# Four operand tiles of an FFN's Strassen products moved by 960 bytes: a longer pad at the end of their pool

## The chip, the cores and the metric

The kernel runs on one core of a Trainium2 chip. The metric is the device time of one execution in microseconds. Three executions of the kernel before took 2714.53, 2717.65 and 2718.61 us; the median, 2717.65 us, is the time that the changed kernel is compared with.

## What is computed

One decoder block in float32: a mixer (sliding-window attention and an mLSTM branch side by side, merged by gates) and a SwiGLU feed-forward network, each behind a modulated RMS norm. The sequence has 2048 tokens of width 1024; the feed-forward width is 2816. The change concerns the first two products of the feed-forward part, `h2 @ w_ffn_gate` and `h2 @ w_ffn_up`:

```
h2 = modulate(rms_norm(x, g_pre_ffn[l]), shift_f, scale_f)
ff = (jax.nn.silu(h2 @ w_ffn_gate[l]) * (h2 @ w_ffn_up[l])) @ w_ffn_down[l]
x = x + gate_f[:, None, :] * rms_norm(ff, g_post_ffn[l])
```

## The kernel before

**Products.** A float32 value is split into a high part (rounded to fp32r by a cast on ScalarE, line 1358) and a low part (the rest, a subtraction on VectorE, line 1359). Each product of two float32 blocks then takes three matmuls: high by high, high by low, low by high.

**Strassen.** The large products are done in Winograd's form of Strassen's method, with seven block products in place of eight. `PROD` (line 1337) lists them as pairs of a weight block and an activation block: ("11","11"), ("S3","T3"), ("S2","T2"), ("22","T4"), ("S1","T1"), ("12","21"), ("S4","22"). S1 to S4 are sums of weight blocks, made on VectorE while the weights are prepared (`a_operands`, lines 1438 to 1466: three sums, lines 1450 to 1452, with the first product of a pair, and S4, line 1461, with the last). T1 to T4 are sums of activation blocks, made once for 1024 tokens by `h_combine` (lines 1380 to 1426), which also splits them.

**The feed-forward part.** Tokens are taken in two halves of 1024 (`b2` = 0 and 1). For each half, `gate_up` (line 1551) runs over eleven pairs of feature tiles, and for each pair over the gate weights and then the up weights; `pair_parts` (line 1468) issues the seven products of one such pair. Each product has four steps of depth 128, and each step three matmuls:

```
for kk in range(4):
    l, r = (hi[:, kk, :], lo[:, kk, :]), tuple(t[:, kk, :] for t in HC[B])
    mm(ps, l[0], r[0], kk == 0 and i in (0, 1, 5), False, True)
    mm(ps, l[0], r[1], False, False, True)
    mm(ps, l[1], r[0], False, kk == 3, True)
```

So a product is 12 matmuls. The weights (`hl`, a double tile of high and low part) are the stationary operand, loaded by TensorE's weight load; the activation rows, 512 float32 or 2048 bytes in each of 128 partitions, are the moving operand. Products 11, S2·T2, S1·T1 and S4·22 add up in a PSUM bank named `acc`, the others in one named `mix`. After a half's `gate_up`, `down` (line 1618) multiplies by `w_ffn_down`; there both operands are `hl` tiles.

**Where the activation blocks lie.** `HC` holds a high and a low tile for each of the seven blocks, `[P, 4, TB]` each: 8192 bytes in each partition, four rows of 2048 bytes. The tiles of 11, 21, 22, T1 and T3 come from the pool `bpool` (name `big`), those of T2 and T4 from a pool of their own, `hcp`, which `open_hc` (line 1364) opens at the right end of SBUF when the mixer's last pool there is closed. Their names are `hcT2h`, `hcT2l`, `hcT4h` and `hcT4l`. Both halves use the same four tiles: they are filled before the first `gate_up`, and again during `down` of the first half. A last small tile, `hc_end`, only takes up room: a pool at the right end grows downwards, so its length sets where the four tiles lie. In the built program they start at bytes 196544, 204736, 212928 and 221120 of a partition, each of which is a multiple of 1024 plus 960. The tiles `big` start at 43008 and every 8192 bytes from there, the tiles `hl` at 26624 and every 4096 bytes from there: all multiples of 1024.

The queues that matter here are TensorE's (matmuls in the order of `PROD`), ScalarE's and VectorE's (splits of the weights up to four products ahead, `ahead=4` in line 1490, and the combination of results in lines 1495 to 1505) and SyncE's, which issues the DMAs.

Of the kernel before, what the change touches and what calls it, by code (L numbers as in the profile page):

```python
# [10 lines left out]
F32 = mybir.dt.float32  # L11
# [8 lines left out]
P = 128  # L20
# [51 lines left out]
def decoder_block(ctx: ExitStack, tc: tile.TileContext, a: dict, out: bass.AP, dbg=None):  # L72
# [664 lines left out]
    def superblock(sb):  # L737
# [475 lines left out]
        def outputs(b):  # L1213
# [24 lines left out]
            def before_m():  # L1238
                end_chunks(NT * (b % 2 + 1))
                load_y(b, 2)  # L1240
                if b + 1 == NBLK:
                    finish(R_ada)
                    open_hc()
                    R["hc"] = spawn(h_combine(0, *HC_FROM_MIXER), L_HC)
# [119 lines left out]
    def open_hc():  # L1364

        p1k.close()
        hcp = ctx.enter_context(tc.tile_pool(name="hcp", bufs=1, side="right", reuse_waits="tile"))
        HC.clear()
        t2h, t2l, t4h, t4l = [hcp.tile([P, 4, TB], F32R, name=f"hc{x}") for x in ("T2h", "T2l", "T4h", "T4l")]
        hcp.tile([P, 8], F32, name="hc_end")  # L1370
        HC["T2"] = [t2h, t2l]
        HC["T4"] = [t4h, t4l]

# [487 lines left out]
```

## Time and profile before

| | us |
|---|---|
| median of three executions | 2717.65 |
| the profiled execution | 2714.22 |
| its span, from the first to the last instruction | 2712.5 |
| TensorE busy in the span | 2641.9 |
| VectorE busy | 1955.8 |
| ScalarE busy | 1303.1 |
| first product with a T2 tile starts at | 1422.0 |
| last matmul with a T4 tile starts at | 2481.5 |

The span is 1.7 us shorter than the profiled execution's own time; the rest lies around it. "Busy" is the time in which an engine had at least one instruction under way. Matmuls overlap: the profile shows a duration for each that is longer than the time until the next one starts, so a run of matmuls is measured from the start of its first to the start of the first one behind it.

### The profile page before, as it was taken

How to read it: one execution, taken by the hardware profiler on the slowest of the kernel's cores; microseconds unless marked ns; L12 is line 12 of the kernel's file. 1: busy time of each engine (PE TensorE's matmuls, PEld its weight loads, DVE VectorE, ACT ScalarE, POOL GpSimd, SP SyncE). 2: the span in 40 equal slices, each digit the busy share in tenths (PEclk: the TensorE clock that was granted, in tenths of full speed). 3: DMA queues.
4: the chain of work that ended last, by engine and by line, in shares of the span. 5: the costliest groups of instructions: out<-in, count | busy, mean ns of one | idle time of the engine just before them, and what ended most of it. 6: DMA issues, size and time to landing. Idle time of an engine off the chain costs nothing.

```text
span 2712.5 us, 35701 instructions
## 1 busy us (share of the span) xinstructions
PE 2641.9 (97%) x12310; PEld 2141.0 (79%) x12310; DVE 1955.8 (72%) x3818; ACT 1303.1 (48%) x2574; POOL 157.8 (6%) x189
## 2 busy tenths in 40 slices
PE   6999999999999999999999999999999999999998
PEld 4867788888886778888878888888777888888886
DVE  7967787777696877776687777776676666666466
ACT  5646544444855654454554433334554333333444
POOL 2010001100101000110000000000000000000000
PEclk8999999999999999999999999999999999999999
DMA  7655346887675643678764454446685232224566
GB/s 250 201 174 172 128 139 200 260 341 253 214 234 161 198 147 119 216 236 300 239 208 166 171 202 149 161 158 223 206 273 184 98 117 95 99 97 148 184 213 217
DMA packets 353638, 511.89 MB, mean 189 GB/s; under 512 B 25120, under 2 KB 213660, under 8 KB 348208
## 3 DMA queue, kind: packets, MB, share of 16 engines
q1 hardware_dynamic: 353456, 509.61, 56.0%
q8 instruction: 97, 1.59, 0.2%
q14 instruction: 85, 0.70, 0.1%
HBM read 357.12 MB, written 144.02 MB: 185 GB/s over the span
## 4 chain that ended last, share of the span: by engine, by line
PE 83%; DVE 8%; DMA 4%; ACT 3%; issue 1%; SPq 0%; POOL 0%; DVEq 0%; ACTq 0%; POOLq 0%
PE acc L204 58%; PE mix L204 24%; PE mix L209 2%; DVE hl L1359 1%; ACT tm L948 1%; DMA raw<-as_d 1%; ACT hl L1358 1%; DMA raw<-in_w_in_dram 1%; DMA big<-big 1%; DVE tm L428 1%; DMA raw<-ws_d 0%; DMA at_d<-tx 0%; DVE big L1359 0%; DVE wlo L260 0%; DMA big<-in_x_dram 0%
## 5 line engine op out<-in xcount | busy, mean ns | idle before, releaser
L204 PE MATMUL acc<-big,hl 128*128 128x512 f32 x3936 | 946.3, 393 | 3.7 <-DVE w L1658 1.7
L204 PEld LDWEIGHTS acc<-big,hl 128*128 128x128 f32 x3936 | 732.7, 188 | 172.5 <-issue 11.4
L1358 ACT CAST hl<-raw 128x512 fp32r<-128x512 f32 x732 | 436.0, 620 | 615.2 <-PE acc L204 384.3
L1359 DVE TENSOR_TENSOR hl<-raw,hl 128x512 fp32r<-128x512 f32 x732 | 494.8, 695 | 255.8 <-ACT hl L1358 249.7
L204 PE MATMUL acc<-whi,big 128*128 128x512 f32 (+1 forms) x1280 | 382.6, 379 | 15.3 <-ACT big L518 8.4
L204 PEld LDWEIGHTS acc<-whi,big 128*128 128x128 f32 x1280 | 237.7, 193 | 59.2 <-ACT big L518 8.5
L204 PE MATMUL mix<-big,hl 128*128 128x512 f32 x1056 | 270.6, 392 | 1.7 <-DVE hl L1359 1.0
L204 PE MATMUL acc<-wlo,big 128*128 128x512 f32 (+1 forms) x640 | 242.6, 381 | 2.8 <-DVE wlo L260 2.8
L204 PE MATMUL acc<-hl,hl 128*128 128x512 f32 x1008 | 237.7, 393 | 6.2 <-DVE hl L1359 3.9
L204 PEld LDWEIGHTS mix<-big,hl 128*128 128x128 f32 x1056 | 198.9, 189 | 45.7 <-DVE hl L1359 1.8
L204 PEld LDWEIGHTS acc<-hl,hl 128*128 128x128 f32 x1008 | 187.0, 188 | 51.9 <-DVE hl L1359 9.3
L204 PE MATMUL mix<-hl,hl 128*128 128x512 f32 x792 | 182.5, 391 | 1.1 <-DVE hl L1359 0.4
L204 PEld LDWEIGHTS mix<-hl,hl 128*128 128x128 f32 x792 | 147.8, 188 | 34.9 <-DVE hl L1359 2.8
L260 DVE TENSOR_TENSOR wlo<-raw,whi 128x1024 fp32r<-128x1024 f32 (+1 forms) x96 | 108.8, 1135 | 69.1 <-ACT whi L259 64.1
L204 PE MATMUL acc<-big,whi 128*128 128x512 f32 x512 | 157.2, 392 | 0.0
L259 ACT CAST whi<-raw 128x1024 fp32r<-128x1024 f32 (+1 forms) x96 | 94.3, 983 | 124.4 <-PE acc L204 108.2
L475 POOL TENSOR_TENSOR rs<-ms,nhalf 128x1 f32<-128x1 f32 (+1 forms) x56 | 53.0, 958 | 1603.1 <-DVE ms L473 1598.0
L204 PEld LDWEIGHTS acc<-wlo,big 128*128 128x128 f32 x640 | 124.0, 194 | 25.6 <-DVE wlo L260 4.2
L204 PE MATMUL acc<-hcT2h,hl 128*128 128x512 f32 x352 | 117.6, 394 | 1.2 <-ACT w L1499 1.2
L204 PE MATMUL mix<-hcT4h,hl 128*128 128x512 f32 x352 | 117.5, 394 | 0.0
L204 PEld LDWEIGHTS acc<-big,whi 128*128 128x128 f32 x512 | 95.7, 188 | 19.5
L204 PE MATMUL acc<-big,wlo 128*128 128x512 f32 x256 | 97.9, 393 | 0.0
(324 smaller groups left out, 3423.3 us busy)
## 6 DMA issues: line engine op xcount, KB each, us to landing
raw<-in_w_in_dram SPq DMA_DIRECT2D x48, 1024.0 KB, 5.4
as_d<-w SPq DMA_DIRECT2D x154, 256.0 KB, 2.0
raw<-as_d SPq DMA_DIRECT2D x70, 512.0 KB, 4.0
raw<-in_w_ffn_gate_dram SPq DMA_DIRECT2D x22, 1024.0 KB, 5.2
raw<-in_w_ffn_up_dram SPq DMA_DIRECT2D x22, 1024.0 KB, 5.8
raw<-ws_d SPq DMA_DIRECT2D x40, 512.0 KB, 4.6
y_d<-tm SPq DMA_DIRECT2D x64, 256.0 KB, 5.5
tx<-in_w_ada_dram SPq DMA_DIRECT2D x64, 256.0 KB, 4.5
```

The costliest lines, as they stand in the source:

```text
L204: T.matmul(o, lhsT=lhsT, rhs=rhs, start=start, stop=stop, skip_group_check=resumed)
L209: T.transpose(o, i, ident[:k, :k])
L259: A.copy(hv, src)
L260: V.tensor_tensor(lv, src, hv.bitcast(F32), op=ALU.subtract)
L428: V.scalar_tensor_tensor(acc, raw[:, k, :], c_, acc, op0=ALU.mult, op1=ALU.add)
L475: G.tensor_tensor(r[:, :n], ms[:, :n], nhalf[:, :n], op=ALU.pow)
L948: A.activation(sc[g][:, j, :], sc[g][:, j, :], AF.Exp, bias=nm_[:, hd:hd + 1], accum_out=sums[:, hd:hd + 1])
L1358: A.copy(v(hi), src)
L1359: V.tensor_tensor(v(lo), src, v(hi).bitcast(F32), op=ALU.subtract)
```

## The change

`hc_end`, the last tile of the pool `hcp`, has 248 float32 per partition in place of 8: 992 bytes in place of 32. Nothing reads or writes it. The four tiles ahead of it start 960 bytes lower, at 195584, 203776, 211968 and 220160, which are multiples of 1024. These four addresses are the only difference between the two built programs: each engine has the same instructions in the same order with the same waits, and all other tiles and the tensors in HBM lie where they lay.

```
@@ -1367,7 +1367,7 @@
         hcp = ctx.enter_context(tc.tile_pool(name="hcp", bufs=1, side="right", reuse_waits="tile"))
         HC.clear()
         t2h, t2l, t4h, t4l = [hcp.tile([P, 4, TB], F32R, name=f"hc{x}") for x in ("T2h", "T2l", "T4h", "T4l")]
-        hcp.tile([P, 8], F32, name="hc_end")
+        hcp.tile([P, 248], F32, name="hc_end")
         HC["T2"] = [t2h, t2l]
         HC["T4"] = [t4h, t4l]
```

More of the change, by code (lines that the diff above doesn't have):

```diff
@@ L1369, in open_hc @@
         t2h, t2l, t4h, t4l = [hcp.tile([P, 4, TB], F32R, name=f"hc{x}") for x in ("T2h", "T2l", "T4h", "T4l")]
-        hcp.tile([P, 8], F32, name="hc_end")
+        hcp.tile([P, 248], F32, name="hc_end")
         HC["T2"] = [t2h, t2l]
```

## The prediction

> **What bounds the kernel now.** I read the page's busy times first, then the chain that ended last, then the two stretches in which the moved tiles are used, and last the tiles themselves. The first two views:
>
> ```profile
> span 2712.5 us, 35701 instructions
> PE 2641.9 (97%) x12310; PEld 2141.0 (79%) x12310; DVE 1955.8 (72%) x3818; ACT 1303.1 (48%) x2574; POOL 157.8 (6%) x189
> ...
> PE 83%; DVE 8%; DMA 4%; ACT 3%; issue 1%; SPq 0%; POOL 0%; DVEq 0%; ACTq 0%; POOLq 0%
> ```
>
> TensorE is busy for 97% of the span and holds 83% of the chain. An average over stages does not say what holds where the change acts, so the next view takes the two stretches of gate and up products alone (the T2 and T4 tiles are moving operands there and nowhere else), and the one after it lists what a matmul waited for in the first of them.
>
> ```profile
> core 0: us, PE busy (x) PEld busy (x) DVE busy (x) ACT busy (x) POOL busy (x), PEclk, DMA share, GB/s
> 1422.00:1829.00 407.00, 407.00 (x1778) 333.48 (x1779) 294.07 (x469) 156.08 (x282) 13.00 (x4) 1.00 0.47 167
> 2072.00:2482.00 410.00, 410.00 (x1793) 335.91 (x1792) 276.80 (x430) 145.96 (x259) 0.34 (x1) 1.00 0.32 108
> ```
>
> ```profile
> engine line waited for: us in total, times, longest us
> PE acc L204 <- ACT w L1499: 1.2, 1, 1.2
> ```
>
> The reader is to see three things. TensorE is busy for every microsecond of both stretches, at a granted clock of 1.00. Its only wait in the first is 1.2 us at the very start. VectorE, the next busiest, works 294.07 us of 407.00. These 817 us are thus bound by the rate at which matmuls follow each other, and by nothing else that the trace shows.
>
> **What sets that rate.** The tile views give the durations of matmuls by moving operand (least, median, most, in ns).
>
> ```profile
> L204 PE MATMUL acc<-hcT2h,hl x352: 393/394/502, 1422.0 to 2478.7; 128*128 128x512 f32 x176
> L204 PE MATMUL acc<-hcT2l,hl x176: 392/394/398, 1422.3 to 2478.4; 128*128 128x512 f32 x176
> L204 PE MATMUL mix<-hcT4h,hl x352: 393/394/398, 1424.9 to 2481.5; 128*128 128x512 f32 x176
> L204 PE MATMUL mix<-hcT4l,hl x176: 393/394/398, 1425.1 to 2481.2; 128*128 128x512 f32 x176
> ...
> L204 PE MATMUL acc<-big,hl x3936: 387/389/796, 209.8 to 2490.9; 128*128 128x512 f32 x197
> L204 PE MATMUL mix<-big,hl x1056: 387/389/628, 1408.6 to 2486.9; 128*128 128x512 f32 x176
> L204 PE MATMUL acc<-hl,hl x1008: 387/389/504, 1835.3 to 2691.9; 128*128 128x512 f32 x168
> L204 PE MATMUL mix<-hl,hl x792: 387/389/501, 1870.2 to 2672.1; 128*128 128x512 f32 x198
> ```
>
> All eight groups have the same shape, type and stationary tile. Four have a median of 389 ns and a least of 387; the four whose moving operand is a T2 or T4 tile have 394 and 392 to 393. Not one of the 1056 on T tiles is as short as the median of the others: this is no scatter. What tells the four apart is where the tile lies: `big` and `hl` start at multiples of 1024 bytes, the T tiles 960 bytes past one. Durations overlap, though, and their ends are modelled, so I take the price from starts. The chain over one pair of gate or up weights merges matmuls that follow each other into the same bank name (start, length, count):
>
> ```profile
> 1458.01 2.80 PE acc L204 x12
> 1460.80 5.09 PE mix L204 x22
> 1465.89 2.72 PE acc L204 x12
> 1468.61 0.45 PE mix L204 x2
> 1469.07 2.72 PE acc L204 x12
> 1471.79 0.45 PE mix L204 x2
> 1472.24 2.72 PE acc L204 x12
> 1474.96 2.27 PE mix L204 x10
> 1477.22 2.80 PE acc L204 x12
> ```
>
> The first piece is S2·T2, the second S22·T4 with ten matmuls on T3's or 21's tiles behind it; the third, fifth and seventh are the products of `acc` on `big` tiles. Twelve matmuls on T2 take 2.80 us, or 233.3 ns each; twelve on `big` take 2.72 us, or 226.7 ns each. The second piece agrees: 5.09 less 2.27 for ten on `big` (the eighth piece) leaves 2.82 us for the twelve on T4. The second half's stretch shows the same lengths at the same places:
>
> ```profile
> 2108.82 2.27 PE mix L204 x10
> 2111.09 2.80 PE acc L204 x12
> 2113.89 5.09 PE mix L204 x22
> ```
>
> **The change part by part.**
>
> *The matmuls on the T tiles.* They are 352 + 176 + 352 + 176 = 1056, or 88 products of 12 (two halves, eleven pairs, gate and up, T2 and T4). At multiples of 1024 I expect them to run like the `big` and `hl` tiles, which lie so: 88 x (2.80 - 2.72) = 88 x 0.08 = **7.0 us less**. With the rounding of both lengths (0.07 to 0.09) that is 6.2 to 7.9 us; by the modelled durations, 1056 x (394 - 389) ns = 5.3 us. At the other end, if the price belongs to something that the move leaves alone (the pool, the far end of SBUF), it is nothing. I take 7.0, since starts are recorded and ends modelled, and since the 6792 matmuls of the other four rows, on tiles at multiples of 1024, agree with each other.
>
> By a rule of the Trainium skill it would be nothing: "TensorE: Matmul & The Clock Gate", section "Wait — 56ns, not 53.3ns?", gives the time from one bf16 matmul to the next, back to back and warm, as the columns over 2.4 GHz and some 2.5 ns more, 215.7 ns at 512, with no term for the operand's address. The trace agrees with it on neither tile group: 226.7 and 233.3 ns stand beside it, in fp32r, and the two differ.
>
> *What lies beside it.* The matmuls follow each other without a wait, so the whole of it is on the path. To be late next, VectorE or ScalarE would have to need more than TensorE: a pair takes 1477.22 - 1458.01 = 19.21 us now and 19.05 after; VectorE's part of it is 294.07 / 407.00 x 19.21 = 13.9 us, ScalarE's 156.08 / 407.00 x 19.21 = 7.4 us, and the DMA engines are at 0.47. Gate and up weights are asked for once in that time, so a pair that is 0.16 us shorter moves no transfer into another's way. If VectorE's cover of 5 us were gone, nothing of the 7.0 us would be left, since TensorE would then run at VectorE's pace.
>
> *The writes into the T tiles.* These are 16 casts and 16 subtractions, 8 of each for each half:
>
> ```profile
> L1358 ACT CAST hcT2h<-tx x4: 613/619/623, 1346.8 to 1383.9; 128x512 fp32r<-128x512 f32 x4
> L1359 DVE TENSOR_TENSOR hcT2l<-tx,hcT2h x4: 681/686/691, 1350.3 to 1386.0; 128x512 fp32r<-128x512 f32 x4
> ...
> L1358 ACT CAST hl<-raw x732: 602/622/654, 208.2 to 2687.5; 128x512 fp32r<-128x512 f32 x183
> L1359 DVE TENSOR_TENSOR hl<-raw,hl x732: 659/687/1524, 209.5 to 2688.2; 128x512 fp32r<-128x512 f32 x183
> ```
>
> A write to a T tile takes what a write to an `hl` tile takes (619 against 622 ns, 686 against 687), so I cost it at nothing. Were all 32 in the path and each moved by the whole 3 ns, it would be 0.1 us either way.
>
> *The weight loads.* Their stationary tiles do not move. The load runs beside the matmul ahead of it:
>
> ```profile
> L204 PEld LDWEIGHTS acc<-hcT2h,hl x352: 186/187/188, 1422.0 to 2478.4; 128*128 128x128 f32 x176
> ...
> L204 PEld LDWEIGHTS acc<-big,hl x3936: 186/188/333, 209.8 to 2490.7; 128*128 128x128 f32 x197
> ```
>
> Beside a matmul of 226.7 ns a load of 188 ns keeps some 39 ns of cover (46 now); nothing comes of it.
>
> *The rest.* The pad is neither read nor written. Instructions, waits and all other addresses stay, so `down`, the mixer and every DMA are as before; they only start earlier, by 3.5 us behind the first half and by 7.0 us behind the second.
>
> **The sum.** The profiled execution goes from 2714.22 to 2707.2 us, its span from 2712.5 to 2705.5. That execution lay 3.4 us under the median of the three, 2717.65; from the median the forecast is **2710.6 us**, 0.26% less. About 0.2% (5.4 us) is what a measurement of this kernel can tell from no change.
>
> **The rivals.**
>
> *The address is not the cause: no change, 2717.65 us.* The T tiles differ from `big` in more than the remainder by 1024: they lie in a pool of their own above all other tiles. If the 6.7 ns belong to that, they stay. For it speaks that no row shows one tile at both kinds of address. Against it, `hl`, from byte 26624, and `big`, up to byte 157696, run alike to the nanosecond, which a price that grows with the address would not leave. The Trainium skill's page "SBUF — State Buffer" stands on this side: "Specifications (TRN2)" names lines of 16 bytes as the grain, and both the old and the new addresses are multiples of 64. "Who interferes with whom" adds that TensorE waits for no other engine there. No row here shows the size of a line.
>
> *The time comes free and is waited away: 2714 to 2717 us.* Place: the hand-over from a product to the splits that later ones need, and then `down`, which waits for DMAs at many places. If one of the two stretches turned out to follow VectorE's or the DMAs' pace, half would be lost: 2717.65 - 3.5 = 2714.1 us. The 407.00 and 410.00 us of unbroken work speak against it.
>
> *The new place collides: slower.* At multiples of 1024 the T tiles share that remainder with the `hl` tiles, which TensorE's weight load reads, and ScalarE and VectorE write, in the same moments. If meeting there cost a matmul as much on top of its present time as the old place costs it, 6.7 ns, the 1056 would give 7.0 us more: 2724.7 us. It decides from 5.4 us / 1056 = 5.1 ns over the present 233.3, that is, where twelve matmuls take over 2.86 us. Against it stands that the `big` tiles share the remainder and the neighbours already, and run at 2.72.
>
> **How the numbers follow.** The forecast gets 0.80, no effect of the address 0.09, gain waited away 0.08, the collision 0.03. The three runs of before lie 4.1 us apart, and the forecast only 1.6 us past the bound of 5.4: of its 0.80 I count 0.05 to "within 0.2%". That gives faster 0.75, same 0.05 + 0.09 + 0.08 = 0.22, slower 0.03. The range goes from the fastest run of before less the largest gain, 2714.53 - 7.9 = 2706.6 us, to the slowest less half the forecast, 2718.61 - 3.5 = 2715.1 us; it takes in most of the waited-away case, and leaves out no effect and the collision, 0.12, with some tails of the forecast.
>
> **What the profile after would show.** Right: the four rows of T2 and T4 at a median of 389 ns and a least of 387; pieces of twelve on T2 of 2.72 us, and of 22 in `mix` of 5.01; both stretches still unbroken and shorter by 3.5 us each. The first is wrong if the rows stay at 394 (the address is not the cause) or rise (collision). The second is wrong if the rows fall to 389 and the pair stays at 19.21 us, with new idle time of TensorE before the splits of lines 1358 and 1359. The forecast of the time is wrong, with all of that right, if `down` gives back more than a microsecond or two in waits for its loads.

## The result and the profile after

The changed kernel took 2706.86 us, the median of six runs (2704.91 to 2708.56), against 2716.30 us for six runs of the kernel before (2711.73 to 2718.61). The ratio is 0.9966, with a 95% interval of 0.9953 to 0.9979: 0.34% faster, or 5.7 to 12.8 us. The profiled execution took 2706.42 us, 7.8 us less than the one of before. One execution of a later run, the one with the pad at 56, took 5071.58 us at a granted clock of 0.89, where the seven others had 0.99, and its ratio and median leave it out.

The head of the page after:

```profile
span 2704.7 us, 35701 instructions
...
PE 2630.0 (97%) x12310; PEld 2139.2 (79%) x12310; DVE 1953.4 (72%) x3818; ACT 1303.3 (48%) x2574; POOL 149.1 (6%) x189
```

The span is 7.8 us shorter, and TensorE's share of it is 97% as before: it does the same 12310 matmuls faster. The chain still runs through TensorE for the most part (82%, before 83%). The matmuls with a moved tile, from the tile views (least, median, most in ns; first and last start in us):

```profile
L204 PE MATMUL acc<-hcT2h,hl x352: 387/389/504, 1421.7 to 2471.0; 128*128 128x512 f32 x176
L204 PE MATMUL acc<-hcT2l,hl x176: 389/389/402, 1422.0 to 2470.8; 128*128 128x512 f32 x176
L204 PE MATMUL mix<-hcT4h,hl x352: 389/389/390, 1424.6 to 2473.7; 128*128 128x512 f32 x176
L204 PE MATMUL mix<-hcT4l,hl x176: 389/389/390, 1424.8 to 2473.5; 128*128 128x512 f32 x176
```

All four medians fell from 394 to 389 ns, the number of the `big` and `hl` tiles. The chain over one pair, as it was shown of before:

```profile
1457.37 2.72 PE acc L204 x12
1460.09 4.99 PE mix L204 x22
1465.08 2.72 PE acc L204 x12
1467.80 0.45 PE mix L204 x2
1468.25 2.72 PE acc L204 x12
1470.97 0.45 PE mix L204 x2
1471.43 2.72 PE acc L204 x12
1474.15 2.27 PE mix L204 x10
1476.41 2.72 PE acc L204 x12
```

Twelve matmuls on T2 take 2.72 us (2.80 before), the 22 in `mix` that begin with T4 4.99 (5.09). A pair takes 1476.41 - 1457.37 = 19.04 us (19.21). The stretches are as unbroken as they were:

```profile
1422.00:1824.00 402.00, 402.00 (x1775) 332.82 (x1774) 292.80 (x467) 156.07 (x281) 3.36 (x4) 1.00 0.48 169
2069.00:2473.00 404.00, 404.00 (x1784) 334.53 (x1783) 275.35 (x428) 145.78 (x258) 0.00 (x0) 1.00 0.32 110
```

**Where the time came from.** By the starts of the matmuls, averaged over the 44 pairs: twelve on T2 went from 2802.3 to 2723.9 ns, twelve on T4 from 2800.0 to 2720.0, and the ten that follow T4's from 2282.2 to 2262.0. The three differences, 78.4 + 80.0 + 20.2 = 178.6 ns, times 44 make 7.9 us; the span is 7.8 us shorter. From the first T2 start to the last T4 start there are 1052.0 us in place of 1059.5: each half's stretch lost 3.9 us, and the part between them, which is mostly `down`, took 0.4 us more. Ahead of the first 0.3 us more were saved, and behind the last nothing. The ten behind T4's in the trace of before:

```profile
1463.44 2.45 PE L204 MATMUL mix<-big,hl 128*128 128x512 f32 x10
1465.73 0.39 PE L204 MATMUL acc<-big,hl 128*128 128x512 f32 x1
```

From their first start to the first start behind them there are 2.29 us, against 2.27 for the other ten of the pair.

So the expected step is there. What no run had shown yet is why: the prediction's "multiples of 1024" is one of several descriptions that fit.

### The profile page after: what moved, and what is told of

It is laid out like the page before. It is cut to its first block, busy times and chain, and to the rows that moved or that the text cites. A ratio compares the mean times of both kernels' runs of the same rounds, so it can differ in the third digit from the quotient of the medians.

```text
span 2704.7 us, 35701 instructions
## 1 busy us (share of the span) xinstructions
PE 2630.0 (97%) x12310; PEld 2139.2 (79%) x12310; DVE 1953.4 (72%) x3818; ACT 1303.3 (48%) x2574; POOL 149.1 (6%) x189
## 4 chain that ended last, share of the span: by engine, by line
PE 82%; DVE 5%; DMA 3%; ACT 3%; issue 1%; POOL 0%; SPq 0%; DVEq 0%; POOLq 0%; ACTq 0%
PE acc L204 57%; PE mix L204 23%; PE mix L209 2%; DVE hl L1359 1%; ACT hl L1358 1%; ACT tm L948 1%; DMA raw<-as_d 1%; DMA raw<-ws_d 0%; DMA at_d<-tx 0%; DVE big L1359 0%; DMA big<-big 0%; DMA raw<-in_w_in_dram 0%; DVE tx L578 0%; DMA raw<-in_w_ffn_down_dram 0%; ACT big L1404 0%
## 5 line engine op out<-in xcount | busy, mean ns | idle before, releaser
L475 POOL TENSOR_TENSOR rs<-ms,nhalf 128x1 f32<-128x1 f32 (+1 forms) x56 | 44.1, 799 | 1603.9 <-DVE ms L473 1602.6
```

The costliest lines, as they stand in the source:

```text
L475: G.tensor_tensor(r[:, :n], ms[:, :n], nhalf[:, :n], op=ALU.pow)
```

## The experiments

The profile of before fits three theories of the place of a moving row. **A**: a row costs 6.7 ns for each piece of 1024 bytes that it touches (two pieces from a multiple of 1024, three from elsewhere). **B**: the grain is finer than 1024. **C**: any start off a multiple of 1024 costs 6.7 ns. Two more came up on the way. **D**: what counts is where the row lies against the weights. **E**: row and weights each pay for their own place. Each ratio below is to runs of the kernel before on the same chip (medians of 2712.18 and 2712.38 us there).

### Matmuls alone

The kernel leaves the decoder block out. It has matmuls, 48 for each case on a source line of its own, over one moving and one weights tile that both start at a multiple of 1024, and then some copies and subtractions:

```
for ps, s, e in run():
    T.matmul(ps[:, :512], lhsT=wt_(0), rhs=mv_(240, 512), start=s, stop=e)  # row 960 bytes on
```

> Leaves the whole decoder block out: matmuls alone, 48 back to back for each case, with the moving operand at various byte offsets from a multiple of 1024 and with 512, 384 or 256 fp32r columns, then weights at various offsets, then subtractions on VectorE and copies on ScalarE at offsets 0 and 960. Theory A (a row costs 6.7 ns for each piece of 1024 bytes that it touches): 512 columns take 226.7 ns at offsets 0 and 1024 and 233.3 at 4, 16, 32, 64, 128, 256, 512, 768, 960 and 1020 alike; 384 columns (1536 bytes) take the same at 0, 256 and 512 (two pieces) and 6.7 ns more at 768 (three); 256 columns take 6.7 ns less at 0 (one piece) than at 256, 512 and 768 (two). Theory B (a finer grain): 512 columns at 512 cost what they cost at 0, and perhaps at 256 and 128. Theory C (any start off a multiple of 1024 costs 6.7 ns, whatever the length): 384 columns at 256 and 512 are as dear as at 768. Weights at another offset: nothing by all three, since the load runs beside the matmul ahead. VectorE and ScalarE: no change expected by any.

Nanoseconds from one start to the next, means of one execution, at a granted clock of 1.00 and with the weights at 0:

| row at | 0 | 4 | 16 | 32 | 64 | 128 | 256 | 512 | 768 | 960 | 1020 | 1024 |
|---|---|---|---|---|---|---|---|---|---|---|---|---|
| 512 columns | 226.7 | 236.6 | 231.8 | 233.4 | 229.1 | 233.3 | 227.0 | 227.7 | 227.2 | 233.1 | 226.7 | 226.9 |

With 384 columns all four offsets gave 173.3 to 173.9, with 256 columns 119.7 to 120.0. With the row at 0, weights at 256, 512 and 768 cost 226.7 to 227.3, but weights at 960 cost 229.0. Rows of the timeline (start, length, twelve matmuls in a bank), line 62 with the row at 960, line 66 at 512:

```profile
66.82 2.96 PE L62 MATMUL bankf<-mv,wt 128*128 128x512 f32 x12
69.62 2.96 PE L62 MATMUL bankg<-mv,wt 128*128 128x512 f32 x12
...
91.83 2.88 PE L66 MATMUL bankg<-mv,wt 128*128 128x512 f32 x12
94.55 2.88 PE L66 MATMUL bankh<-mv,wt 128*128 128x512 f32 x12
```

Starts are 2.80 us apart at 960 and 2.72 at 512. The kernel's price came back by itself, with no other engine at work while these rows ran. Theories A and C fall: 256, 512 and 768 are free, and at 768 the row of 384 columns touches three pieces and costs no more. B is what is left, with a grain of 256; but a row at 1020 was free too, at 226.7, and no theory had that. And the weights' place counts, which no theory had either. Copies on ScalarE (617 ns) and subtractions on VectorE (692 to 693 ns) were the same at 0 and 960.

### Four offsets in the kernel

```
+        for x, gap in (("T2h", 16), ("T2l", 32), ("T4h", 64), ("T4l", 120)):
+            hcs.append(hcp.tile([P, 4, TB], F32R, name=f"hc{x}"))
+            hcp.tile([P, gap], F32, name=f"hc_gap{x}")
```

> The four T tiles at 64, 128, 256 and 512 bytes past a multiple of 1024 (T2h, T2l, T4h, T4l). Theories A and C: all four stay at 233.3 ns, the time is that of before (2716 us, within 1 us). Theory B: T4l at 512 falls to 226.7 (176 matmuls, 1.2 us less), and perhaps T4h at 256 (352, 2.3 us less) and T2l at 128 (1.2 us less).

The ratio was 0.9991 (0.9980 to 1.0002), an interval that holds no change; the rows decide here:

```profile
L204 PE MATMUL acc<-hcT2h,hl x352: 388/396/501, 1419.7 to 2471.1; 128*128 128x512 f32 x176
L204 PE MATMUL acc<-hcT2l,hl x176: 391/395/395, 1420.1 to 2470.9; 128*128 128x512 f32 x176
L204 PE MATMUL mix<-hcT4h,hl x352: 389/389/401, 1422.6 to 2473.9; 128*128 128x512 f32 x176
L204 PE MATMUL mix<-hcT4l,hl x176: 389/389/395, 1422.9 to 2473.7; 128*128 128x512 f32 x176
```

T4 at 256 and 512 runs like `big`, T2 at 64 and 128 does not. In the kernel too, a multiple of 256 will do.

### T2 alone

```
-        t2h, t2l, t4h, t4l = [hcp.tile([P, 4, TB], F32R, name=f"hc{x}") for x in ("T2h", "T2l", "T4h", "T4l")]
+        t2h, t2l = [hcp.tile([P, 4, TB], F32R, name=f"hc{x}") for x in ("T2h", "T2l")]
+        hcp.tile([P, 240], F32, name="hc_gap")
+        t4h, t4l = [hcp.tile([P, 4, TB], F32R, name=f"hc{x}") for x in ("T4h", "T4l")]
```

> The T2 tiles at multiples of 1024, the T4 tiles 960 past one, as before. If each row pays for its own place: twelve matmuls on T2 take 2.72 us, on T4 2.80 us, and the time is half way, 88 / 2 x 0.08 = 3.5 us under before (2712.8 of 2716.3). Rival, that the pool as a whole or the meeting of neighbours counts: both groups move together, to 2.72 or to 2.80, and the time is that of after or of before.

```profile
L204 PE MATMUL acc<-hcT2h,hl x352: 389/389/499, 1425.9 to 2478.0; 128*128 128x512 f32 x176
...
L204 PE MATMUL mix<-hcT4h,hl x352: 394/394/394, 1428.8 to 2480.8; 128*128 128x512 f32 x176
```

T2 is at 389 and T4 at 394, each by its own place; a pair took 19.14 us, between the 19.21 of before and the 19.04 of after. The ratio, 0.9989 (0.9975 to 1.0003), or 3.0 us, agrees with the 3.5 expected, though its interval also holds no change. The pool and its end of SBUF are cleared: its tiles went apart.

### The big tiles at 64

```
+    pre = ctx.enter_context(tc.tile_pool(name="pre", bufs=1))
+    pre.tile([P, 16], F32, name="pre_pad")
     bpool = ctx.enter_context(tc.tile_pool(name="bpool", bufs=14))
```

> The changed kernel with a pad of 64 bytes ahead of the pool of the big tiles, which puts these, and the tm, tx and w tiles behind them, 64 bytes past a multiple of 1024 (tx: 64 more than before); the T tiles stay at multiples of 1024. Theory A or C: 4992 matmuls on big tiles of 512 columns go from 226.7 to 233.3 ns, of them 2652 behind 1408 us, where TensorE waits for little (17.7 us), and 2364 ahead of it, where it may wait (0 to 15.8 us): 2706.9 + 17.7 to 33.5, so 2724.6 to 2740 us, while the T tiles keep 226.7. Rival (the price belongs to the pool of the T tiles): big stays at 226.7 and the time at 2706.9.

The ratio was 1.0053 (1.0034 to 1.0071). The traced span is 18.0 us over that of the changed kernel, at the low end of the 17.7 to 33.5 expected; the two ratios to before, 1.0053 and 0.9966, lie some 24 us apart, in its middle. The size for a matmul was off: a product on `big` took 2.75 us, 229 ns a matmul, as an offset of 64 did in the first run, and not 2.80. Nor did T2 keep its 2.72: its product, right behind ten matmuls on `big`, took 2.77, while T4's twelve averaged 2.72. And another group paid that was not expected to (both tile rows had a median of 389 before):

```profile
1467.92 2.77 PE acc L206 x12
1470.69 5.03 PE mix L206 x22
1475.71 2.75 PE acc L206 x12
...
L206 PE MATMUL acc<-big,hl x3936: 387/392/797, 211.4 to 2500.3; 128*128 128x512 f32 x197
L206 PE MATMUL acc<-whi,big x1280: 278/394/796, 26.4 to 1420.1; 128*128 128x512 f32 x147, 128*128 128x264 f32 x36
```

In the last row `whi` is the moving operand and had not moved; `big`, now at 64, holds the weights. Row 0 against weights 64 costs what the T tiles' row 960 against weights 0 did. That led to theory D: 0 - 64 and 960 - 0 leave the same remainder, 192, by 256.

### The pad at 56

```
-        hcp.tile([P, 8], F32, name="hc_end")
+        hcp.tile([P, 56], F32, name="hc_end")
```

> The end pad 192 bytes longer in place of 960: the T tiles lie 768 past a multiple of 1024, a multiple of 256 alone. Grain of 256 (the earlier runs gave 226.8 to 227.7 ns at 256, 512 and 768): twelve matmuls on T2 in 2.72 us, the pair in 19.04 us, the time that of the change as made, 7 to 9 us under before. Grain of 1024, the rule in the change's title: 2.80 us, the pair 19.22, the time of before.

```profile
1458.10 2.72 PE acc L204 x12
1460.82 4.99 PE mix L204 x22
...
1477.13 2.72 PE acc L204 x12
```

The pair takes 19.03 us, and the ratio is 0.9967 (0.9956 to 0.9979): the whole gain of the change, with the tiles 192 bytes lower in place of 960.

### All pools at the left 64 bytes lower

```
-    const.tile([P, 24], F32, name="const_end")
+    const.tile([P, 8], F32, name="const_end")
```

> The kernel before with a pad 64 bytes shorter ahead of all pools at the left: weights (hl, whi, wlo), big, tm and w tiles lie 960 past a multiple of 1024, as the T tiles do. Nothing is aligned any more. Theory D (what counts is where the moving row lies against the weights that are loaded beside it, by the remainder of 256): all differences are nought, every large matmul takes 226.7 ns, the T tiles' too, the pair 19.04 us, and the time is 7 to 9 us under before. Theory E (each operand pays for its own place): over 4992 matmuls on big tiles go to 229 to 235 ns as well, the pair takes 19.3 to 19.7 us, and the time is 6 to 35 us over before.

This is the run that parts D from E. The T tiles lie where they lay before, 960 past a multiple of 1024, and now their weights do too:

```profile
L204 PE MATMUL acc<-big,hl x3936: 387/389/798, 210.6 to 2479.9; 128*128 128x512 f32 x197
L204 PE MATMUL mix<-big,hl x1056: 388/389/501, 1406.5 to 2475.9; 128*128 128x512 f32 x176
...
L204 PE MATMUL acc<-hcT2h,hl x352: 389/389/497, 1418.4 to 2467.8; 128*128 128x512 f32 x176
L204 PE MATMUL mix<-hcT4h,hl x352: 389/389/389, 1421.3 to 2470.5; 128*128 128x512 f32 x176
```

None of these tiles is aligned, and every group is at 389. The pair takes 19.04 us, and from the first T2 start to the last T4 start there are 2470.5 - 1418.4 = 1052.1 us, as after the change. Theory E falls. The ratio, 0.9987 (0.9977 to 0.9997), is 3.5 us under before, less than the 7 to 9 expected; the median, 2707.56 us, lies 4.6 over the 2702.93 of the run with the pad at 56 on the same chip. This pad also moves the constants, the small tiles and the mixer's tiles, and the traced execution, at 2703.54 us the fastest of its ten, does not show what gave the rest back; that stays open.

### The T tiles apart from their weights

The same edit as in the run before, made on the changed kernel.

> The changed kernel with the same shorter pad: the T tiles at multiples of 1024, weights and big tiles 960 past one. Theory D: the T matmuls alone differ from their weights, by 0 - 192, which is 64 modulo 256; an offset of 64 cost 2.3 ns in the first run of matmuls alone and in the run with the big tiles at 64, so twelve on T2 take 2.75 us and the pair 19.10, a time some 2.5 us over that of the change. Theory E: T at 226.7 or 229, the matmuls on big at 229 to 235, the pair 19.3 to 19.6 us.

```profile
1456.21 2.76 PE acc L204 x12
1458.98 5.06 PE mix L204 x22
1464.04 2.72 PE acc L204 x12
...
1475.38 2.76 PE acc L204 x12
```

The T tiles lie at multiples of 1024, as the change has them, and yet twelve on T2 take 2.76 us and not 2.72; the products on `big`, at 960 with weights at 960, take 2.72. The pair takes 19.17 us, more than the 19.10 expected: the first matmuls after each change between the two kinds of place are slower still. The ratio was 1.0003 (0.9993 to 1.0013). Not all of that is the T tiles' place, since the 4.6 us that this pad costs by itself, still open, are in it. Against the run before, which has the same pad and the T tiles level with their weights, the median rose by 5.4 us, to 2712.92, and the traced stretch from the first T2 start to the last T4 start by 5.0, to 1057.1. That is what parting them costs here, and the tiles lie as the change put them.

### Pairs of offsets, matmuls alone

This kernel is like the first one, with 72 matmuls for each pair of offsets, and was executed once.

> Leaves the whole decoder block out: matmuls of 512 fp32r columns alone, 72 back to back for each pair of offsets of the moving row and of the weights. Theory D: 226.7 ns wherever both have the same offset (4, 32, 64, 128, 192 and 960), weights at w with the row at 0 cost what the row at 256 - w costs with the weights at 0 (weights 64 like row 192, weights 192 like row 64, weights 252 like row 4), row 64 with weights 128 like row 192, row 128 with weights 64 like row 64. Theory E: equal offsets cost the sum of both, up to 240 ns, and 64 beside 128 more than either alone.

| row, weights | ns | row, weights | ns |
|---|---|---|---|
| 0, 0 | 226.7 | 0, 64 | 233.4 |
| 32, 32 | 227.4 | 192, 0 | 233.4 |
| 64, 64 | 227.0 | 64, 128 | 233.4 |
| 128, 128 | 227.3 | 64, 0 | 229.0 |
| 192, 192 | 227.3 | 128, 64 | 229.2 |
| 960, 960 | 226.7 | 0, 192 | 233.3 |
| 4, 4 | 237.7 | 252, 0 | 226.9 |
| 0, 4 | 232.4 | 0, 252 | 233.3 |

Line 84 has both at 960, line 92 the row at 32 and the weights at 0:

```profile
275.11 2.88 PE L84 MATMUL banka<-mv,wt 128*128 128x512 f32 x12
277.83 2.88 PE L84 MATMUL bankb<-mv,wt 128*128 128x512 f32 x12
...
343.86 2.96 PE L92 MATMUL bankb<-mv,wt 128*128 128x512 f32 x12
346.66 2.96 PE L92 MATMUL bankc<-mv,wt 128*128 128x512 f32 x12
```

Equal offsets of 32 bytes and more are free, and pairs with one difference cost the same (64 beside 128 like 0 beside 64; 128 beside 64 like 64 beside 0). Theory D misses at four places: equal offsets of 4 cost 237.7; a row at 252 costs nothing, where weights at 4 cost 232.4; weights at 252 cost 233.3, where a row at 4 cost 236.6 in the first run; and weights at 192 cost 233.3, where a row at 64 costs 229.0. The first three have an offset that is no multiple of 32, so the rule is shown for multiples of 32 alone.

### Fewer weight columns

> Leaves the whole decoder block out: matmuls of 512 fp32r columns alone, 72 back to back for each case, with weights of 128, 64 and 32 columns, and at 128 columns a list of offsets of the row and of the weights. If the price comes from the weight load that reads beside the moving row, fewer weight columns cost less: 233.3 ns at (row 960, weights 0) with 128 columns, some 230 with 64 and 228 or less with 32, against 226.7 at (0, 0). Rival, that the load's length does not count (the moving row is read more slowly for its place against the weights' start): 233.3 at all three widths. Period: with the row at 0, weights at 192 and 704 cost 233.3 and at 448 and 960 cost 229.0 if differences repeat every 512 bytes; 233.3, 233.3, 233.3 and 229.0 if every 1024; all alike if every 256.

This kernel is like the one before, and was executed once too. At (row 960, weights 0): 233.3 ns with 128 columns of weights, 232.6 with 64, 231.7 with 32. At (0, 0): 226.7, 230.0 and 231.6. The view with both at 0 and 32 columns has starts 2.78 us apart, where 128 columns have 2.72:

```profile
226.61 2.94 PE L78 MATMUL bankh<-mv,wt 128*32 128x512 f32 x12
229.39 2.94 PE L78 MATMUL banka<-mv,wt 128*32 128x512 f32 x12
```

The load did get shorter (188, 134 and 108 ns), but (960, 0) did not fall to the 228 or less that was expected of a price set by its length. What falls is the difference between the places, and mostly because the free case is lost: 6.6 ns between (960, 0) and (0, 0) with 128 columns, 2.6 with 64 and 0.1 with 32. Five pairs of offsets were run at each width; with 32 columns all five lie between 230.7 and 231.7. So the simple form of that theory falls, and that the load has a part in it does not. With 128 columns, weights at 192, 448, 704 and 960 beside a row at 0 all cost 229 here, rows at these four offsets beside weights at 0 all 233.3, and 448 beside 192 costs 226.7: the difference counts by its remainder of 256. Weights at 192 cost 233.3 in the run before and 229.1 in this one, so some pairs have two rates, and what picks one is not known. So the rule is shown and its mechanism is not: whether the two reads meet in SBUF or inside TensorE, no run here decides, nor whether a matmul's own weights count or the next ones, which are loaded while it runs; in every case both lay alike.

## Why the prediction was right, and where its reason was not

- **The bound.** TensorE was to run without a break in both stretches; it did so after the change, and 7.8 of the 7.9 us saved on matmuls reached the span. The rival that the gain is waited away fell; `down` took 0.4 us more between the halves.
- **88 x 0.08 = 7.0 us.** Measured by starts, 78 and 80 ns per pair, or 7.0 us in all. The term was right to a tenth.
- **What was missing.** The ten matmuls behind T4's became 20 ns shorter per pair too, 0.9 us in all. The trace of before had them, in 5.09 - 2.27 = 2.82 against 2.80, where the prediction read 2.82 as agreement. In that trace the first five matmuls after the step from T4 to `big` run at 226 to 236 ns, and then the pace is 227. So the 22 in `mix` take 4.99 us after and not the 5.01 forecast, and each half's stretch is 3.9 us shorter and not 3.5.
- **The median** fell by 9.4 us, the traced execution by 7.8. The interval, 5.7 to 12.8, holds both, and the forecast of 7.0; the six runs of before lie up to 7 us apart, so the 1.6 us between the two are no finding. The median of 2706.86 us lies 3.7 under the forecast of 2710.6 and only 0.3 above the low end of the range, 2706.6. Most of that is not the matmuls: the forecast started from a median of three runs, 3.4 us above the traced one, and after the change the traced run lies 0.4 from the median. For the traced run 2707.2 was forecast and 2706.42 measured. That the median stayed within the range was in part luck.
- **The weight loads** were costed at nothing since "their stationary tiles do not move". The loads' length did stay. But their address is one half of the price: the step was right in its sum and wrong in what it took for irrelevant.
- **"At multiples of 1024 I expect them to run like the `big` and `hl` tiles, which lie so."** The outcome was as forecast, and the condition was not the one that counts. A remainder of 768 gives the same gain, equal remainders of 960 give the fast matmuls with nothing aligned, and multiples of 1024 beside weights at 960 lose two thirds of it (5.0 of the 7.5 us between the first T2 start and the last T4 start). What counts, for 512 columns of fp32r and 128 columns of weights, is the difference between row and weights: with both at multiples of 32 bytes, every pair tried that differs by a multiple of 256 is free, and no other is. The prediction argued from tiles that share two properties, aligned and level with their weights, and named the first. That the change brought the second along was luck.
- **No effect of the address**, the rival with the Trainium skill at its side ("SBUF — State Buffer", "Specifications (TRN2)", lines of 16 bytes): it fell. Offsets of 32, 64 and 128 bytes, all multiples of 16, cost 2.4 to 6.7 ns, so a line of 16 bytes does not describe this price. The Trainium skill's other sentence there ("Who interferes with whom"), that TensorE waits for no other engine, is not touched: the price is there with TensorE alone.
- **The collision**, held to be unlikely, was argued the wrong way round: sharing the remainder with the weights is what makes the tiles fast.

## What to carry to other kernels

When TensorE has no gaps, list the matmul's duration by moving tile and compare groups of one shape: 5 ns between medians, with not one matmul of the slower group as short as the median of the faster, is a cause and not scatter. For matmuls like these (fp32r, 512 columns, 128 columns of weights), place moving and stationary tiles so that their addresses differ by a multiple of 256 bytes; putting all of them at multiples of 256 does it. Before a rule is drawn from "these tiles are aligned and fast", move the partner as well as the tile.

## What the runs showed of the hardware

- In the first run of matmuls alone, fp32r back to back took 120.0, 173.3 and 226.7 ns for 256, 384 and 512 columns: 53.3 ns for each 128 columns, and 13.3 ns beside them.
- The place of a row of 512 columns against its weights was worth up to 11 ns of 226.7, or 5% (237.7 with both at 4). For 256 and 384 columns only multiples of 256 were tried, which were free.
- With weights of 64 or 32 columns, matmuls with both operands at 0 were 3 to 5 ns slower than with 128. At the places that cost something with 128 columns (229.0 to 233.3 ns), they lay between 228.4 and 232.6; with 32 columns the place hardly counted.
